# The first 1024 rows of x laid out as parts of 256 and 768 rows instead of one part, with a store for each

## The chip, the cores and the metric

The kernel runs on one core of one Trainium2 chip. The metric is device time in microseconds (us) of one execution; several runs are taken and their median is given. A profiled execution has, beside its time, a span: the time from the first to the last instruction that the profile shows.

## The reference

```python
def setup_inputs():
    batch, seq, d_model, r = 16, 512, 768, 16
    ...
        "x": np.random.randn(batch, seq, d_model).astype(np.float32),
        "A": np.random.randn(d_model, r).astype(np.float32) * 0.1,
        "B": np.random.randn(r, d_model).astype(np.float32) * 0.1,
        "scale": 0.5,

def reference(x, A, B, scale):
    lora = np.matmul(np.matmul(x, A), B)
    return (x + scale * lora).astype(np.float32)
```

x has 16 x 512 = 8192 rows of 768 floats: 25.17 MB that must be read, and as much that must be written. A and B are 48 KB each.

## The kernel before, in words

**Tiles, parts and groups.** A tile is 128 rows of x, one for each partition. There are 64 tiles. `PARTS` (L14) says how they lie in memory: a part of S tiles is a run of 128 x S rows of x, and partition p holds the rows p*S to p*S+S-1 of that run (`memory`, L96). One partition's share of a part is thus one contiguous run of S x 3072 bytes, and the shares of neighbouring partitions follow each other. A transfer of n of the S tiles takes n x 3072 bytes out of each share. The parts are 8, 8, 16, 16 and 16 tiles. In the core's memory the buffer `x_sb` has room for 48 tiles (`ROOM`, L61), and the last part takes the place of the first two (`tiles`, L103).

**Transfers.** `LOADS` (L106) and `STORES` (L128) list them as (part, first tile, tiles). There are eight loads: of part 0 the first 2 tiles (load 0) and then the other 6 (load 1), part 1 whole (load 2), part 2 in two halves (loads 3 and 4), part 3 whole (load 5), and part 4 in two halves (loads 6 and 7). There are five stores, one for each part. All are issued by SyncE (`on_sync`, L135), whose queue is SP in the profile: loads 0 and 1, the small A and B, and loads 2 to 5 at the start. Then SP waits until the sums of group 1 are done and until the fifth pair of matrix products into `lora` is under way (L169), issues stores 0 and 1 back to back (L170 and L171), waits for the landing of store 0 (`s_out0`, L172), issues load 6 into the place that store 0 read, waits for store 1 (`s_out1`, L174) and issues load 7 into the place of store 1. The stores of parts 2, 3 and 4 follow, each when its last group is summed (L176 to L178).

**Work on a group.** Eight tiles are a group; there are eight groups. ScalarE casts the first four tiles of a group to fp16 (`narrowed`, L182), GpSimd the other four; in group 0 GpSimd takes tiles 0 and 1, which load 0 brings, and ScalarE the others, which load 1 brings. VectorE transposes the group in 32 x 32 blocks (L246), TensorE multiplies by A (`projected`, L277), ScalarE scales the small product and spreads it (L234), TensorE multiplies by B (`raised`, L298), and VectorE adds the result to x in place (`summed`, L251), two tiles in each of 32 additions. `STORED` (L130) lists the group after which each store may leave; the waits on `s_sum` are counted by it. The order on each engine is that of the program, with counting semaphores between the engines. A semaphore that a transfer raises gets 16 from it.

**The end.** GpSimd waits for all the sums (L339) and for the last three stores (L341, 16 for each), and then clears the semaphores.

Of the kernel before, what the change touches and what calls it, by code (L numbers as in the profile page):

```python
# [10 lines left out]

PARTS = [8, 8, 16, 16, 16]  # L14


GROUP = 8
# [11 lines left out]
def kernel(  # L29
# [8 lines left out]
    nc = tc.nc  # L38
# [9 lines left out]
    NC = D // 64  # L48
    NG = sum(PARTS) // GROUP
    PAIRS = GROUP // 2  # L50
    assert sum(PARTS) * P == T and NG * GROUP == sum(PARTS)
    sc = float(scale)


    def sb(name, shape, dtype):
        return nc.alloc_sbuf_tensor(name, shape, dtype).ap()
# [3 lines left out]

    ROOM = sum(PARTS[:-1])  # L61
    x_all = sb("x_sb", [P, ROOM, D], fp32)
# [20 lines left out]
    def sem(name):  # L83
        sems.append(nc.alloc_semaphore(name))
        return sems[-1]
# [4 lines left out]
    tok = 0  # L90
    for i, S in enumerate(PARTS):
        parts.append(tok)
# [3 lines left out]
    def memory(t2, i, s, n):  # L96
        S = PARTS[i]
        return t2[ds(parts[i], S * P), :].rearrange("(p s) d -> p s d", s=S)[:, ds(s, n), :]

    def held(i, s, n):  # L100
        return tiles(where.index((i, s)), n)

    def tiles(t, n):  # L103
        return x_all[:, ds(t % ROOM, n), :]

    LOADS = [  # L106
        (0, 0, 2), (0, 2, 6), (1, 0, 8), (2, 0, 8), (2, 8, 8), (3, 0, 16), (4, 0, 8), (4, 8, 8)
    ]
    s_load = [sem(f"s_load{k}") for k in range(len(LOADS))]

# [12 lines left out]
    s_out0, s_out1 = sem("s_out0"), sem("s_out1")  # L123

    s_sum, s_out = sem("s_sum"), sem("s_out")

    MMS = 2 * NC
    STORES = [(0, 0, 8), (1, 0, 8), (2, 0, 16), (3, 0, 16), (4, 0, 16)]  # L128

    STORED = [where.index((i, s + n - 1)) // GROUP for i, s, n in STORES]  # L130

    section = ExitStack()
    section.enter_context(tc.tile_critical(no_gpsimd_drain=True))  # L133

    def on_sync(e):  # L135
        def load(k):
            ld = LOADS[k]
            e.dma_start(out=held(*ld), in_=memory(x2, *ld)).then_inc(s_load[k], 16)  # L138

        def summed(k):  # L140
            e.wait_ge(s_sum, k + 1)
            if STORED[k] + 1 < NG:

                e.sem_inc(s_free[PAIRS - 1], 1)

        def store(k, done):
            st = STORES[k]
            e.dma_start(out=memory(out2, *st), in_=held(*st)).then_inc(done, 16)

        load(0)  # L150
        load(1)
        e.wait_ge(s_ready, 1)
        blocks = A.rearrange("(c e) r -> c (e r)", e=64)
        for c in range(SETS):
            e.dma_start(
                out=a_rows[c : SET * SET : SET, :], in_=blocks[ds(c * SET, SET), :]
            ).then_inc(s_a, 16)
        e.wait_ge(s_brows, 1)
        e.dma_start(out=b_rows[0 : R * APART : APART, :], in_=B).then_inc(s_b, 16)
        for k in range(2, len(LOADS) - 2):  # L160
            load(k)

        for p in range(2, PAIRS):
            e.sem_inc(s_free[p], 1)
        summed(0)
        summed(1)


        e.wait_ge(s_lora, 2 * PAIRS + 2)  # L169
        store(0, s_out0)  # L170
        store(1, s_out1)  # L171
        e.wait_ge(s_out0, 16)  # L172
        load(len(LOADS) - 2)
        e.wait_ge(s_out1, 16)  # L174
        load(len(LOADS) - 1)
        for k in range(2, len(STORES)):  # L176
            summed(k)
            store(k, s_out)  # L178

    here = set()  # L180

# [55 lines left out]
    def on_vector(e):  # L237
# [10 lines left out]
        def summed(g, p):  # L248
            xs = tiles(g * GROUP + 2 * p, 2)
            e.wait_ge(s_lora, g * PAIRS + p + 1)  # L250
            ins = e.tensor_tensor(out=xs, in0=xs, in1=lora[p % 2], op=mybir.AluOpType.add)  # L251
            if p + 1 == PAIRS and g in STORED:
                ins.then_inc(s_sum, 1)
# [15 lines left out]
    def on_tensor(e):  # L269
# [57 lines left out]
        for p in range(PAIRS):  # L327
            raised(p)

    on_sync(nc.sync)  # L330
    on_gpsimd(nc.gpsimd)
    on_scalar(nc.scalar)
# [5 lines left out]

    nc.gpsimd.wait_ge(s_sum, len(STORED))  # L339
    nc.gpsimd.sem_clear(range(nums[0], s_sum.num))  # L340
    nc.gpsimd.wait_ge(s_out, (len(STORES) - 2) * 16)  # L341
    nc.gpsimd.sem_clear(range(s_sum.num, s_out.num + 1))
    section.close()

# [34 lines left out]
```

## Time and profile before

| | |
|---|---|
| median of 3 runs | 123.59 us (123.59 to 123.83) |
| the profiled execution | 123.66 us |
| its span | 121.8 us |
| VectorE busy | 81.8 us, 67% of the span |
| TensorE matmul busy | 52.8 us, 43% |
| ScalarE busy | 37.5 us, 31% |
| GpSimd busy | 28.4 us, 23% |
| bytes moved | 50.43 MB: 25.26 read from HBM, 25.17 written |

The profile divides the span into 40 equal slices and gives each engine's busy share in tenths; the row DMA is the mean busy share of the 16 DMA engines that serve the core. A packet is one contiguous piece of a transfer, on one DMA engine. The chain of waits follows the work back from the last instruction that an engine executed. The time from issue to landing of a transfer includes its stay in the queue behind other transfers.

### The profile page before, as it was taken

How to read it: one execution, taken by the hardware profiler on the slowest of the kernel's cores; microseconds unless marked ns; L12 is line 12 of the kernel's file. 1: busy time of each engine (PE TensorE's matmuls, PEld its weight loads, DVE VectorE, ACT ScalarE, POOL GpSimd, SP SyncE). 2: the span in 40 equal slices, each digit the busy share in tenths (PEclk: the TensorE clock that was granted, in tenths of full speed). 3: DMA queues.
4: the chain of work that ended last, by engine and by line, in shares of the span. 5: the costliest groups of instructions: out<-in, count | busy, mean ns of one | idle time of the engine just before them, and what ended most of it. 6: DMA issues, size and time to landing. Idle time of an engine off the chain costs nothing.

```text
span 121.8 us, 885 instructions
## 1 busy us (share of the span) xinstructions
PE 52.8 (43%) x322; PEld 31.0 (25%) x322; DVE 81.8 (67%) x42; ACT 37.5 (31%) x43; POOL 28.4 (23%) x24
## 2 busy tenths in 40 slices
PE   0000239487457547746745736994474540000000
PEld 0000026254233324424423312662233310000000
DVE  0002950699999999999999979969998795000000
ACT  4003938535408402835340093534004000000000
POOL 7731647135008002605300080530000000000000
PEclk9999999999999999999999995589999999555555
DMA  3999999999997996999999999997997998998990
GB/s 56 426 436 422 452 428 411 452 428 411 500 500 339 452 516 299 436 428 436 452 403 436 436 420 436 468 500 323 468 516 339 436 516 371 403 516 371 403 516 0
DMA packets 1928, 50.43 MB, mean 414 GB/s; under 512 B 236, under 2 KB 236, under 8 KB 392
## 3 DMA queue, kind: packets, MB, share of 16 engines
q1 hardware_dynamic: 1928, 50.43, 96.9%
HBM read 25.26 MB, written 25.17 MB: 414 GB/s over the span
## 4 chain that ended last, share of the span: by engine, by line
DVE 50%; PE 14%; issue 8%; DMA 8%; ACT 3%; SPq 0%
DVE x_sb L251 32%; DVE xt L246 18%; PE ps_yt L277 8%; DMA x_sb<-in_x_dram 8%; PE lora_ps L298 5%; ACT xn L190 3%; SPq L138 0%; SPq L374 0%; SPq L133 0%
## 5 line engine op out<-in xcount | busy, mean ns | idle before, releaser
L251 DVE TENSOR_TENSOR x_sb<-x_sb,lora_ps 128x1536 f32<-128x1536 f32 x32 | 53.8, 1737 | 2.5 <-PE lora_ps L298 2.5
L298 PE MATMUL lora_ps<-b_mm,y_bd 128*128 128x512 f16 (+1 forms) x128 | 26.3, 342 | 22.4 <-issue 13.4
L190 ACT CAST xn<-x_sb 128x3072 f16<-128x3072 f32 (+1 forms) x9 | 23.4, 2609 | 36.7 <-DMA x_sb<-in_x_dram 24.1
L277 PE MATMUL ps_yt<-xt,w_bd 128*128 128x256 f16 x192 | 27.3, 297 | 11.6 <-DVE xt L246 11.6
L190 POOL CAST xn<-x_sb 128x3072 f16<-128x3072 f32 (+1 forms) x8 | 20.7, 2588 | 45.3 <-DMA x_sb<-in_x_dram 23.0
L246 DVE STREAM_TRANSPOSE xt<-xn 128x3072 f32<-128x3072 f32 (+1 forms) x9 | 27.1, 3008 | 6.2 <-PE ps_yt L277 5.3
L277 PEld LDWEIGHTS ps_yt<-xt,w_bd 128*128 128x128 f16 x192 | 19.6, 104 | 20.0 <-issue 14.7
L298 PEld LDWEIGHTS lora_ps<-b_mm,y_bd 128*128 128x128 f16 x128 | 11.3, 101 | 35.5 <-issue 18.2
L234 ACT ACTIVATE y_bd<-ps_yt 32x256 f16<-32x256 f32 x32 | 12.0, 375 | 19.2 <-PE ps_yt L277 18.9
L239 DVE STREAM_TRANSPOSE a_t<-a_rows 32x1024 f32<-32x1024 f32 x1 | 2.0, 1965 | 11.5 <-DMA a_rows<-in_A_dram 11.5
L310 PE MATMUL lora_ps<-b_half,pick 128*128 128x512 f16 (+1 forms) x2 | 0.8, 504 | 12.8 <-POOL b_half L208 12.8
L310 PEld LDWEIGHTS lora_ps<-b_half,pick 128*128 128x128 f16 x2 | 0.1, 103 | 12.8 <-issue 12.8
L216 POOL COPY w_bd<-w_one 32x384 f16<-32x384 f16 x4 | 2.0, 502 | 0.2
L208 POOL CAST b_half<-b_rows 128x768 f16<-128x768 f32 x1 | 0.8, 829 | 4.7 <-DMA b_rows<-in_B_dram 4.7
L190 ACT ACT_TABLE_LOAD x1 | 1.3, 1283 | 0.9 <-SPq L133 0.9
L198 POOL MEMSET w_bd<- 128x1536 f32 x1 | 1.4, 1373 | 0.0
L210 POOL CAST w_one<-a_t 32x384 f16<-32x384 f32 x1 | 0.9, 852 | 0.9 <-DVE a_t L239 0.9
L195 POOL MEMSET a_rows<- 32x1024 f32 x1 | 0.9, 942 | 0.5 <-SPq L133 0.5
L227 ACT CAST b_mm<-lora_ps 128x768 f16<-128x768 f32 x1 | 0.8, 799 | 0.0
L196 POOL MEMSET b_rows<- 128x768 f32 x1 | 0.7, 728 | 0.0
L199 POOL MEMSET y_bd<- 128x512 f32 x1 | 0.5, 516 | 0.0
L201 POOL TENSOR_SCALAR_AFFINE_SELECT pick<-pick 128x128 f16<-128x128 f16 x1 | 0.3, 300 | 0.0
(5 smaller groups left out, 0.6 us busy)
## 6 DMA issues: line engine op xcount, KB each, us to landing
out_dram<-x_sb SPq DMA_DIRECT2D x3, 6144.0 KB, 22.3
x_sb<-in_x_dram SPq DMA_DIRECT2D x5, 3072.0 KB, 14.6
x_sb<-in_x_dram SPq DMA_DIRECT2D x1, 6144.0 KB, 41.8
out_dram<-x_sb SPq DMA_DIRECT2D x2, 3072.0 KB, 14.3
x_sb<-in_x_dram SPq DMA_DIRECT2D x1, 2304.0 KB, 9.8
x_sb<-in_x_dram SPq DMA_DIRECT2D x1, 768.0 KB, 4.6
a_rows<-in_A_dram SPq DMA_DIRECT2D x3, 16.0 KB
b_rows<-in_B_dram SPq DMA_DIRECT2D x1, 48.0 KB, 7.7
```

The costliest lines, as they stand in the source:

```text
L190: ins = copy(out=xn[:, ds(first, n), :], in_=tiles(t, n))
L195: e.memset(a_rows[0:Q], 0.0).then_inc(s_ready, 1)
L198: e.memset(w_bd.rearrange("p c k m -> p (c k m)").bitcast(fp32), 0.0)
L210: e.tensor_copy(out=w_one.rearrange("i (c e) k r -> i c e (k r)", c=SETS), in_=a_t[0:Q].rearrange("i k r (e c) -> i c e (k r)", c=SET)[:, ...
L216: e.tensor_copy(out=w_bd[ds(b * Q, Q), :, :, ds(b * Q, R)], in_=w_one).then_inc(s_w, 1)
L234: last = e.mul(out=y_bd[q, :, q], in_=y_ps[q, :, :], mul=sc)
L239: e.transpose(out=a_t[0:Q].rearrange("i k r c -> i (k r) c"), in_=a_rows[0:Q].rearrange("c (i k r) -> c (k r) i", k=2, r=R),).then_inc(s_r ...
L246: return e.transpose(out=ts[0], in_=ts[1])
L251: ins = e.tensor_tensor(out=xs, in0=xs, in1=lora[p % 2], op=mybir.AluOpType.add)
L277: mm = e.matmul(y_ps, w_bd[:, c, k, :], xv[:, :, c, :, k], start=(m == 0), stop=(m == MMS - 1),)
L298: mms.append(e.matmul(t[:, k, ds(n0, w)], y_bd[:, 2 * p + k, :], b_mm[:, ds(n0, w)], start=True, stop=True,))
L310: last = e.matmul(lora[0][:, 0, ds(n0, w)], pick.rearrange("p b r -> p (b r)"), b_half[:, ds(n0, w)], start=True, stop=True,)
```

## The change

Part 0 becomes two parts: the 2 tiles that load 0 brings and the 6 that load 1 brings. There are six parts, so the numbers of the later ones go up by one; the tiles' places in `x_sb`, the groups, and the eight loads with their sizes and their order stay. The rows that a tile of the first eight stands for are others, and so are the addresses in HBM that these transfers touch: load 0 reads one run of 768 KB and load 1 one of 2304 KB, where both took pieces of 6 KB and 18 KB out of shares of 24 KB. The store of part 0 becomes two, of 6 tiles and of 2 tiles, issued in this order, both counted on `s_out0`; SP waits for 32 there before load 6. The store of the next 8 tiles is issued right behind the two, as before behind one. What the first two stores wait for is one entry of `STORED`, so the counts on `s_sum` are as before.

```diff
-PARTS = [8, 8, 16, 16, 16]
+PARTS = [2, 6, 8, 16, 16, 16]
...
     LOADS = [
-        (0, 0, 2), (0, 2, 6), (1, 0, 8), (2, 0, 8), (2, 8, 8), (3, 0, 16), (4, 0, 8), (4, 8, 8)
+        (0, 0, 2), (1, 0, 6), (2, 0, 8), (3, 0, 8), (3, 8, 8), (4, 0, 16), (5, 0, 8), (5, 8, 8)
     ]
...
-    STORES = [(0, 0, 8), (1, 0, 8), (2, 0, 16), (3, 0, 16), (4, 0, 16)]
+
+    STORES = [(1, 0, 6), (0, 0, 2), (2, 0, 8), (3, 0, 16), (4, 0, 16), (5, 0, 16)]
 
     STORED = [where.index((i, s + n - 1)) // GROUP for i, s, n in STORES]
+    assert STORED[0] == STORED[1]
+    STORED = STORED[1:]
...
         e.wait_ge(s_lora, 2 * PAIRS + 2)
         store(0, s_out0)
-        store(1, s_out1)
-        e.wait_ge(s_out0, 16)
+        store(1, s_out0)
+        store(2, s_out1)
+        e.wait_ge(s_out0, 32)
         load(len(LOADS) - 2)
         e.wait_ge(s_out1, 16)
         load(len(LOADS) - 1)
-        for k in range(2, len(STORES)):
+        for k in range(2, len(STORED)):
             summed(k)
-            store(k, s_out)
+            store(k + 1, s_out)
...
-    nc.gpsimd.wait_ge(s_out, (len(STORES) - 2) * 16)
+    nc.gpsimd.wait_ge(s_out, (len(STORES) - 3) * 16)
```

## The prediction

> **What bounds the kernel now.** I read the slices and the DMA queue first, since 50.43 MB in a span of 121.8 us is a mean of 414 GB/s.
>
> ```profile
> DMA  3999999999997996999999999997997998998990
> DMA packets 1928, 50.43 MB, mean 414 GB/s; under 512 B 236, under 2 KB 236, under 8 KB 392
> q1 hardware_dynamic: 1928, 50.43, 96.9%
> ```
>
> The 16 DMA engines are busy for 96.9% of the span: from the second slice to the last but one nothing is left over. A share of 96.9% is 118.0 us, so only 3.8 us of the span, lead and tail together, lie outside. The stretches say whether the rate differs between reading and writing (columns: the stretch and its length, busy time and instructions of PE, PEld, DVE, ACT, POOL, granted clock, DMA share, GB/s).
>
> ```profile
> 2.00:4.00 2.00, 0.00 (x0) 0.00 (x0) 0.00 (x0) 0.20 (x1) 2.00 (x4) 1.00 0.88 255
> 10.00:18.00 8.00, 1.48 (x6) 0.64 (x7) 5.40 (x3) 4.93 (x3) 3.69 (x6) 1.00 1.04 442
> 47.50:55.50 8.00, 4.29 (x28) 2.37 (x26) 8.00 (x5) 4.25 (x5) 2.75 (x1) 1.00 1.02 439
> 0.00:121.80 121.80, 52.85 (x322) 30.99 (x322) 81.85 (x42) 37.48 (x43) 28.45 (x24) 0.90 0.97 414
> ```
>
> Loads run at 442 GB/s (10 to 18 us), stores at 439 (47.5 to 55.5): the same ceiling. Only the start is slower, 255 GB/s from 2 to 4 us, though the engines are 88% busy there: the first packets of load 0 take long. Third comes the chain of waits, in order of time; its last two pieces:
>
> ```profile
> 95.32 0.02 issue
> 95.34 6.75 DVE x_sb L251 x4
> ```
>
> The chain gives DVE 50% of the span, but it ends at 102.09 us, where the last store leaves. What follows, 20 us, is a transfer. SP's own line of time shows how late that issue is:
>
> ```profile
> 44.42 0.82 SPq L148 DMA_DIRECT2D out_dram<-x_sb  x2
> 55.26 7.75 SPq L138 DMA_DIRECT2D x_sb<-in_x_dram  x2
> ...
> 102.12 0.33 SPq L148 DMA_DIRECT2D out_dram<-x_sb  x1
> ```
>
> The packet records of the trace, set from the start of the span, have the first packet of the last store at 104.99 us and its last end at 120.46. Load 0 was issued at 0.97 and its first packet ran at 1.98, so an issue needs 1.0 us to become a packet; the last store could have run at 103.1 and stood 1.9 us in the queue. Even at the end VectorE has 1.9 us to spare. The time is thus 1.98 us of lead, 118.5 us of packets without a gap, 1.3 us of tail, and 1.86 us that the profiled execution (123.66) has outside its span. Only what changes the packets' time, or opens a gap, counts.
>
> **What a packet costs.** Each transfer of x has 128 packets, 8 for each DMA engine. By the packet records their medians are 234 ns for 6 KB (load 0), 686 for 18 KB (load 1), 912 for 24 KB (store 0), 1815 for 48 KB (last store). From 24 to 48 KB, 24,576 bytes cost 903 ns; 24 KB by that rate leave 9 ns of fixed cost, and 9 + 677 = 686 and 9 + 226 = 235 fit the small ones. A packet that raises a semaphore takes 9 ns too.
>
> **The change, part by part.**
>
> The loads. Number, size and order are as before; only addresses in HBM differ. The steady 6 KB packet already runs at 234 ns, the ceiling less 9 ns, though it is cut out of shares of 24 KB; so a contiguous run gives nothing there. What is left is the start: the mean of load 0's 128 packets is 316 ns, 82 over the steady one, 8 x 82 = 0.66 us for each engine. Of the first 16 packets 13 take 490 to 996 ns, with nothing ahead of them; of the last 64 nearly all take 234. If the old addresses cause this, 0.66 us is saved; if the new ones are as much worse, 0.66 us is lost. I take 0, because most of the excess stands in the first packet of an engine, which has nothing to overlap with at any address. Load 1 (mean 692 against 686) has 0.05 us to give.
>
> The stores. 128 packets of 24 KB become 128 of 18 KB and 128 of 6 KB: 686 + 234 - 912 = 8 ns for each partition, 0.064 us for an engine's eight, and one more semaphore packet, 0.009: **+0.07 us**. No store of 6 KB packets is in this trace. The low end is a packet without fixed cost, 0. The high end is load 0's mean for all of them: (316 + 692 - 912) x 8 = 0.77 us. I take the steady value, since stores of 24 KB (912) and loads of 24 KB (916) are within 4 ns.
>
> The third issue on SP. Three issues stand where two took 0.82 us, so the store of the next 8 tiles is issued 0.41 us later, at 45.24 instead of 44.83. Ahead of it stand the two new stores, 8 x (686 + 234) = 7.4 us of packets, and the end of load 5: it costs nothing. Without that cover it would cost 0.41 us. Behind it on SP is only the wait for `s_out0`.
>
> The wait for 32. It ends when the 2 tiles have landed, 0.07 us later than 55.26. Load 6 hangs on it, then load 7 and the later stores. Behind the awaited bytes the queue holds the 8-tile store, 8 x 912 ns = 7.3 us, which hides the new packets' 0.07 us and the issue. If that cover were gone, issue to packet would cost 1.0 us. Load 6 gates the casts of group 6:
>
> ```profile
> 69.91 2.75 ACT L190 CAST xn<-x_sb 128x3072 f16<-128x3072 f32 x1 [7.25 <-DMA x_sb<-in_x_dram]
> ```
>
> and VectorE waited 0.68 us for GpSimd's half of it, so the sums and the last issue are 0.07 us late too, out of a slack of 1.9.
>
> Sum: +0.07 us on 123.66 for the profiled kind of execution, **123.73**; on the median 123.59 (0.07 below the profiled one) **123.66 us**. No change that can be told: 0.2%, about 0.25 us, is what a measurement of this kernel can tell, and the three runs shown are 0.24 apart.
>
> A rule speaks against the new small store: the Trainium skill, "DMA: Bandwidth & Descriptors", section "Rules for kernel authors", asks for at least 1 MiB in a DMA, and its section "Anatomy of one DMA — SWDGE (gpsimd) path" fits 2.0 us fixed for each. By it one more DMA would give an estimate of 123.59 + 2.0 = 125.6 us, where the row above gives 0.07. The trace disagrees with it as a cost in a full queue: packets of load 1 start at 4.56 us while those of load 0 end until 5.26.
>
> **Rivals.**
>
> *The start gets slower* (slower). Neighbouring DMA engines, four partitions apart, read load 0 from addresses 24 KB apart instead of 96 KB. If the first packets collide more, the excess of 0.66 us doubles, all later packets move with it, and the time is 123.66 + 0.66 = 124.3 us. It decides from +0.25 us, when load 0's packets average about 345 ns. For it: the start is the only place below the ceiling. Against it: each engine has several packets in a row at 234 ns soon after.
>
> *The start gets faster* (faster). The same excess is due to the scattered rows and falls to between nothing and a half. Half gone: 123.66 - 0.33 = 123.3; all gone: 123.0. For it: later packets of load 0 too are at times 300 to 870 ns. Against it: those are few, and the steady ones show no cost of scatter.
>
> *The small store is slow* (slower). Its 6 KB packets cost load 0's mean, not 234: +0.77 us in all, 124.4 us. For it: no such write is seen, and the only 6 KB packets here were slow on the mean. Against it: those were at an idle queue, and these stand behind 18 KB packets.
>
> *Each DMA has a fixed price that shows* (slower). Issue to landing of load 0 is 4.6 us and its 786,432 bytes at 439 GB/s are 1.8, so 2.8 us are fixed. If the new landing exposed that, 126.4 us. Against it are the covers of 7.3 us above.
>
> ```profile
> out_dram<-x_sb SPq DMA_DIRECT2D x2, 3072.0 KB, 14.3
> x_sb<-in_x_dram SPq DMA_DIRECT2D x1, 2304.0 KB, 9.8
> x_sb<-in_x_dram SPq DMA_DIRECT2D x1, 768.0 KB, 4.6
> ```
>
> **How the numbers follow.** No change 0.46; faster start 0.25; slower start 0.16; slow small store 0.11; fixed price 0.02. So faster 0.25, same 0.46, slower 0.29. The start alone has 41% of the doubt because its excess has no explanation in the trace. The time is the likeliest case's, 123.66, with a range of its own from 123.4 to 123.9. The range over the cases goes from a start with most of its excess gone (123.66 - 0.56) to the two slower ones: 123.1 to 124.4. It leaves out a start wholly cured, both slower causes at once and the exposed price.
>
> **What would show it.** 2072 packets instead of 1928 (128 + 16 more), 252 under 512 B, 536 under 8 KB; DMA busy for 118.1 us of the span; the longest wait of SP for a store shorter by 0.34 us (0.41 less at its start, 0.07 more at its end); loads 6 and 7 issued from 55.3; 6 KB store packets at 234 ns. A rate in the stretch from 2 to 4 us far from 255 GB/s would be a changed start. I am wrong if a gap opens around 45 to 56 us, if those packets are slower, or if the last store is issued later than 104 us.

## The result, and the profile after

The changed kernel takes 124.51 us (median of 9 runs, 124.36 to 125.17); the kernel before, run beside it, 123.81 (9 runs, 123.59 to 124.16). The ratio is 1.006 with a 95% interval of 1.004 to 1.0081: slower by about 0.7 us. The prediction was no change, 123.66, with a range up to 124.4.

The slices and the queue of the changed kernel:

```profile
DMA  3999999999999898999999999999999899899890
DMA packets 2072, 50.43 MB, mean 411 GB/s; under 512 B 252, under 2 KB 252, under 8 KB 536
q1 hardware_dynamic: 2072, 50.43, 96.6%
```

The packet counts are the forecast ones, 144 more, all under 8 KB. The span is 122.7 us instead of 121.8, and the DMA engines are still busy for 96.6% of it. So no gap has opened that would hold 0.9 us: the packets themselves take longer. SP's line of time shows nothing late in the issues:

```profile
43.87 1.32 SPq L151 DMA_DIRECT2D out_dram<-x_sb  x3
55.38 7.73 SPq L141 DMA_DIRECT2D x_sb<-in_x_dram  x2
63.23 38.12 SPq L151 DMA_DIRECT2D out_dram<-x_sb  x3
```

The last store is issued at 101.0 us, a microsecond earlier than before, and ends later. The stretches show where the packets lose. The two last columns are the DMA share and the GB/s; the GB/s divided by the share is the rate of the DMA engines while they are busy. The kernel before, around the three places where the queue goes from loading to storing or back, called turns here:

```profile
45.00:48.00 3.00, 2.15 (x16) 1.39 (x16) 3.00 (x3) 0.01 (x1) 0.00 (x0) 1.00 1.02 434
60.00:63.00 3.00, 1.33 (x12) 0.84 (x11) 3.00 (x3) 1.50 (x4) 0.00 (x0) 1.00 0.97 410
74.00:78.00 4.00, 3.68 (x14) 1.98 (x15) 4.00 (x3) 0.66 (x2) 0.40 (x1) 0.50 1.04 430
```

The changed kernel, the start and the same three places:

```profile
2.00:4.00 2.00, 0.00 (x0) 0.00 (x0) 0.00 (x0) 0.19 (x1) 2.00 (x4) 1.00 0.88 326
45.00:48.00 3.00, 2.32 (x16) 1.39 (x16) 3.00 (x3) 0.00 (x0) 0.00 (x0) 1.00 0.75 309
60.00:63.00 3.00, 1.33 (x9) 0.54 (x7) 3.00 (x2) 1.50 (x4) 0.00 (x0) 1.00 1.01 401
74.00:78.00 4.00, 2.97 (x21) 1.81 (x22) 4.00 (x3) 0.34 (x1) 0.00 (x0) 1.00 1.10 412
```

The start is faster: 326 GB/s where it was 255. But a busy DMA engine's rate falls at each turn: from 434/1.02 = 425 to 309/0.75 = 412, from 423 to 397, and most around 76 us, from 413 to 375. The packet records say how much that is. The table gives, for each DMA engine, the time that its eight packets of a transfer take beyond the steady price (235 ns for 6 KB, 686 for 18, 913 for 24, 1816 for 48), and where the last engine ends; each kernel was profiled twice.

```
us over the steady price     before   again   after   again
load 0                        0.65     0.63    0.27    0.44
load 1                        0.05     0.04    0.12    0.09
load 5 (turn A, 45 us)        0.05     0.27    0.17    0.13
8-tile store (turn B, 60 us)  0.03     0.12    0.19    0.22
load 7 (turn C, 75 us)        0.16     0.25    0.56    0.70
packets of all, us          118.05   118.37  118.49  118.76
end of the last engine      120.46   121.03  121.42  121.53
```

All other transfers stay within 0.06 of their price. Apart from the start, the slow packets are the last ones ahead of a turn: in load 7 of the changed kernel 22 packets of 128 take up to 1651 ns instead of 913. On the mean of two profiles the packets take 0.41 us more for each engine, and the last engine falls behind by another 0.3: 0.7 us, the measured loss.

### The profile page after: what moved, and what is told of

It is laid out like the page before. It is cut to its first block, busy times and chain, and to the rows that moved or that the text cites. A ratio compares the mean times of both kernels' runs of the same rounds, so it can differ in the third digit from the quotient of the medians.

```text
span 122.7 us, 886 instructions
## 1 busy us (share of the span) xinstructions
PE 50.4 (41%) x322; PEld 29.5 (24%) x322; DVE 81.7 (67%) x42; ACT 37.5 (31%) x43; POOL 28.4 (23%) x24
## 3 DMA queue, kind: packets, MB, share of 16 engines
q1 hardware_dynamic: 2072, 50.43, 96.6%
## 4 chain that ended last, share of the span: by engine, by line
DVE 33%; DMA 29%; PE 9%; issue 4%; ACT 3%; POOL 2%; SPq 1%; DVEq 0%
DVE x_sb L255 21%; DMA x_sb<-in_x_dram 20%; DVE xt L250 12%; DMA out_dram<-x_sb 9%; PE ps_yt L281 6%; ACT xn L194 3%; PE lora_ps L302 3%; POOL xn L194 2%; SPq L141 0%; SPq L151 0%; SPq L378 0%; DVEq L268 0%; SPq L136 0%
## 5 line engine op out<-in xcount | busy, mean ns | idle before, releaser
L302 PE MATMUL lora_ps<-b_mm,y_bd 128*128 128x512 f16 (+1 forms) x128 | 25.0, 327 | 24.4 <-issue 15.9
L281 PE MATMUL ps_yt<-xt,w_bd 128*128 128x256 f16 x192 | 25.7, 286 | 11.4 <-DVE xt L250 11.4
L281 PEld LDWEIGHTS ps_yt<-xt,w_bd 128*128 128x128 f16 x192 | 18.8, 101 | 19.1 <-issue 14.6
L302 PEld LDWEIGHTS lora_ps<-b_mm,y_bd 128*128 128x128 f16 x128 | 10.5, 97 | 37.3 <-issue 17.9
```

The source lines that it names most:

```text
L281: mm = e.matmul(y_ps, w_bd[:, c, k, :], xv[:, :, c, :, k], start=(m == 0), stop=(m == MMS - 1),)
L302: mms.append(e.matmul(t[:, k, ds(n0, w)], y_bd[:, 2 * p + k, :], b_mm[:, ds(n0, w)], start=True, stop=True,))
```

## The experiments

Theories that the runs are to tell apart are named S, L and so on in the expectations.

**The split store alone, the new loads alone.** First kernel: the old parts and loads, with

```diff
-    STORES = [(0, 0, 8), (1, 0, 8), ...
+    STORES = [(0, 2, 6), (0, 0, 2), (1, 0, 8), ...
```

> Old parts and loads; only the first store is split into 6 and 2 tiles, now pieces of 18 KB and 6 KB out of shares of 24 KB. Theory S (the split store brings the loss, through the packets around the later turns between loading and storing): 124.3 to 124.6 us, and the 24 KB packets of load 7 average over 960 ns as in the changed kernel (983), not 933 as before. Theory L (the new addresses of the first loads bring it, by shifting the DMA engines against each other from the start on): within 0.15 us of the kernel before, load 7 near 933 ns, because the split itself costs 0.07 us.

Second: loads 0 and 1 from contiguous runs, the stores as before.

```diff
-in_=memory(x2, *ld)
+in_=run(x2, k) if k < 2 else memory(x2, *ld)
```

> The first 8 tiles are loaded as two contiguous runs, as in the changed kernel, but leave as one store in shares of 24 KB, so 1024 rows of the output stand in other places. Theory L: 124.3 to 124.6 us, load 7 over 960 ns. Theory S: no slower than before, 123.3 to 123.8 us, since load 0's packets average 269 ns instead of 316, 0.38 us less for each DMA engine; load 7 near 933 ns.

Measured: the split store 124.19 us, ratio 1.0023 (1.0008 to 1.0038); the new loads 124.71, ratio 1.0066 (1.0043 to 1.0089). Load 7 of the first lies 0.27 us over its price, of the second 0.82. So the loads alone bring as much as the whole change, as theory L has it, though load 0's packets got quicker. The split store's own packets cost what was forecast, 0.06 us for each engine: 234 ns for 6 KB, 687 for 18 KB. But the kernel with the split alone is 0.23% slower, 0.28 us, where theory L allowed 0.15. Its trace has 0.25 us at turn A, about what the second trace of the kernel before has, and no run shows where the rest of its loss lies. The two losses don't add up to that of the change. The stretch around turn C of the second kernel, at 387/1.10 = 352:

```profile
74.00:78.00 4.00, 3.05 (x14) 1.63 (x15) 4.00 (x2) 0.83 (x3) 0.00 (x0) 0.69 1.10 387
```

**Both kernels once more**, for second traces.

> The kernel before once more, for a second trace. If the slow packets at the turns are a trait of the kernel, load 7 averages 915 to 950 ns again and all packets together take 118.0 to 118.2 us for each engine. If they are chance of one execution, the mean of load 7 may as well be near 980.

> The changed kernel once more, for a second trace. If a trait: load 7 at 960 to 1000 ns, 118.4 to 118.6 us of packets for each engine, and the last engine about 1 us behind the median one. If chance: load 7 near 930 and the loss elsewhere.

They took 124.08 and 124.59 us and are the columns "again" above. Turn C looks like a trait, on two traces each: 0.16 and 0.25 before, 0.56 and 0.70 after. But the kernel before moves too. Its second execution issued the stores at 43.87 us instead of 44.42 and lost 0.27 us at turn A, not 0.05; its packets took 118.37 us, above what I expected.

**The turn without the other transfer in the queue.** In the changed kernel SP waits for load 7 before it issues the next store.

```diff
         load(len(LOADS) - 1)
+        e.wait_ge(s_load[len(LOADS) - 1], 16)
```

> The changed kernel, with SP waiting for load 7's landing before it issues the store of the next part, so that no store stands in the queue while load 7 ends. Theory M (the last packets before a turn are slow because the DMA engines that are done already move the next transfer the other way): load 7's mean falls from 983 and 1001 ns to 912 to 920, no packet over 1000 ns; a gap of 1 to 2 us opens behind it, of which the 0.6 to 0.7 us saved pays a part: 124.9 to 126.0 us. Rival R (they are slow from something else at that time, VectorE or the place read): load 7 stays over 960 ns, and the time is 125.5 us or more.

132.32 us, ratio 1.0647 (1.0589 to 1.0705), a miss of mine: SP also releases TensorE's buffers in `summed`, so VectorE stood still from 67 to 80 us, and the run couldn't tell M from R. Load 7 had no slow packet. The mended form puts the wait behind that release:

```diff
             summed(k)
+            if k == 2:
+                e.wait_ge(s_load[len(LOADS) - 1], 16)
             store(k + 1, s_out)
```

> The changed kernel, with the store of the part behind load 7 issued only when load 7 has landed, but SP's release to TensorE, which the earlier form of this held back too, given at its usual time: the sums run on while load 7 ends. Theory M (packets ahead of a turn are slow because the queue already holds the transfer the other way): load 7's mean 912 to 920 ns, none over 1000, and the turn between loads and stores costs a gap of 1 to 2.5 us instead of 0.6 us: 125 to 126.5 us. Rival R (VectorE's and the other engines' work slows them): over 960 ns.

125.54 us, ratio 1.0126 (1.0091 to 1.0162); load 7's mean is 912.3 ns, its slowest packet 922, with VectorE at work throughout:

```profile
74.00:76.00 2.00, 0.87 (x4) 0.52 (x5) 2.00 (x1) 1.01 (x3) 0.00 (x0) 0.80 0.91 393
76.00:78.00 2.00, 2.00 (x8) 0.96 (x7) 2.00 (x2) 0.00 (x0) 0.00 (x0) 0.50 0.20 86
```

The rate while busy is 432, and the gap stands behind it. Theory M holds this far: the last packets of load 7 are slow only when the store already stands in the queue behind them, and the other engines' work doesn't slow them.

**Load 0 alone, load 1 alone** contiguous. In these two some rows are read twice and others not at all.

```diff
+in_=run(x2, k) if k == 0 else memory(x2, *ld)     (the other: k == 1)
```

> The kernel before, with load 0 alone reading a contiguous run of 768 KB; load 1 reads its old pieces, so some rows are read twice and some not at all. Theory P0 (what counts is the first packets: the quicker start sets the DMA engines against each other in another way): 124.3 us or more, load 7 over 960 ns. Theory P1 (it is load 1's addresses): as before, 123.6 to 123.9 us, load 7 near 940 ns.

> The kernel before, with load 1 alone reading a contiguous run of 2304 KB, load 0 its old pieces. Theory P1: 124.3 us or more, load 7 over 960 ns. Theory P0: as before, 123.6 to 123.9 us, load 7 near 940 ns.

Load 0 alone: 124.26 us, ratio 1.0026 (1.0000 to 1.0053), load 7 at 972 ns. Load 1 alone: 123.83 us, ratio 1.0000 (0.9973 to 1.0027), load 7 at 951. They point to the first transfer, as P0 has it, but weakly: the two intervals overlap, and load 0 alone costs only four tenths of what both do together. In its trace load 0 gains 0.34 us of packets and load 1 loses 0.33.

**The standing of the DMA engines.** By standing I mean how far the 16 engines are apart in the queue. The semaphore packets behind loads 2, 3 and 4 show it: in the traces of the two kernels the first and the last engine are 0.7 to 0.8 us apart at 18 us, and as far apart at 32 us, so the start sets it. I changed it first by loading A in one transfer, so that it puts one packet on each of 12 engines instead of three on each of four:

```diff
-        for c in range(SETS):
-            e.dma_start(out=a_rows[c : SET * SET : SET, :], in_=blocks[ds(c * SET, SET), :]...
+        e.dma_start(out=a_rows[0:NC, :], in_=blocks).then_inc(s_a, 16)
```

> The kernel before, with the small A in one transfer of 12 rows instead of three of 4 rows: each of the three puts a 4 KB packet on four DMA engines only. If what the turns cost hangs on how the DMA engines stand to each other (P0 in the wide sense), this moves it too, in either direction, by 0.2 us or more on load 7's packets or the end. If only the first loads' addresses count, the turns stay as before and the time falls by at most 0.3 us, the two packets less on the busiest engines.

> The changed kernel, with the small A in one transfer of 12 rows instead of three of 4. Theory P (what counts is how the DMA engines stand to each other after the start, not the addresses): the turns change again, load 7's mean falls below 950 ns, and the time to 124.2 us or less. Rival A (the contiguous addresses as such): load 7 stays over 960 ns, 124.4 us or more.

> The changed kernel with A in one transfer, once more, for a second trace. If its quick turns were its trait: load 7 again below 960 ns, the 24 KB store near 914, the last packets of load 5 near 1819. If chance: one of them back at the changed kernel's values (load 7 983 to 1001, the store 937 to 940, load 5 1832 to 1837).

On the kernel before: 124.15 us, ratio 1.0014 (0.9991 to 1.0037); 0.5 us is lost on load 2, and turns A and C cost 0.03 and 0.17. The turns hardly moved, against the expectation. On the changed kernel: 124.07 us, ratio 1.0023 (1.0006 to 1.0041). Its load 0 is quick, and its turns are cheap: A, B and C cost 0.03, 0.01 and 0.25, in the second trace 0.09, 0.01 and 0.30. So the addresses as such don't make the turns dear. But that second execution took 124.54 us, as long as the changed kernel: both traces lose 0.47 and 0.42 us on load 2, and their packets take 118.53 and 118.49 us for each engine, no less than the changed kernel's. With A in one transfer the change costs a difference of ratios of 0.0009, 0.1 us, close to what I forecast for it; the two intervals overlap.

**A small transfer ahead of load 0**, to take the slow first packets off it with the old addresses.

```diff
+        e.dma_start(out=xt[:, 0, 0:256].bitcast(fp32), in_=x2[0:P, 0:128]).then_inc(s_warm, 16)
         load(0)
```

> The kernel before with its old addresses, and ahead of load 0 a small transfer of 128 pieces of 512 bytes that nothing uses (VectorE waits for it once, at the start). It takes the slow first packets upon itself, so load 0's packets should average below 280 ns (316 before), as in the changed kernel. Its own cost is one issue, 0.4 us, and 0.1 to 0.3 us of packets. Theory P (a quick load 0 sets the engines so that the turns cost more): load 7's mean over 960 ns, 124.6 us or more. Rival A (the contiguous addresses as such): load 7 at 930 to 950 ns, 124.1 to 124.5 us.

It couldn't tell the theories apart: load 0's packets averaged 337 ns, not below 280, so the start was no quicker. 124.92 us, ratio 1.0079 (1.0049 to 1.0108). Of this, 2.4 us of the profiled execution lie outside the span, where other kernels have 1.8; that I can't explain. It does show that the slow packets of load 0 aren't only the first of an idle queue: with pieces 24 KB apart they stay slow, and a contiguous run cures part of it.

**The standing wiped out.** In both kernels the first stores are issued only when load 5 has landed, so that all engines run dry and start together.

```diff
-        e.wait_ge(s_lora, 2 * PAIRS + 2)
+        e.wait_ge(s_load[len(LOADS) - 3], 16)
```

> The changed kernel, with the first stores issued only when load 5 has landed, so that all DMA engines run dry once and start the stores together. Theory P (the loss is carried by how far the DMA engines stand apart since the start): load 7's mean falls from 983 and 1001 ns to below 930, and the engines end within 0.4 us of each other instead of 1.6; the gap itself costs 1.5 to 2 us, so 124.6 to 125.4 us, within 0.2 us of the unchanged kernel treated in the same way. Rival N (not the standing of the engines but the contiguous run at the start, in some other way): load 7 over 960 ns, 0.5 us or more behind the unchanged kernel treated so.

> The kernel before with the same wait for load 5's landing. Theory P: load 7 below 930 ns, ends within 0.4 us, 124.5 to 125.3 us, at most 0.2 us from the changed kernel so treated. Rival N: the same here, but 0.5 us or more ahead of it.

126.77 us for the changed kernel, ratio 1.0225 (1.0194 to 1.0255), and 126.71 for the unchanged one, 1.0227 (1.0196 to 1.0257). So treated, the two kernels differ by 0.06 us, which counts against rival N, though the intervals would allow about 0.5 us. But the rest of my expectation was the wrong way round: the turns got dearer, not cheaper. At turn B, to which the engines came 0.15 us apart, it cost 0.77 and 0.74 us; at turn C, 0.50 and 0.24 apart, 1.02 and 0.86, with up to 38 slow packets. Turn A, whose stores were issued after the load had landed, cost 0.03 in both. The changed kernel so treated, around its turn C, at 393/1.15 = 342:

```profile
77.00:80.00 3.00, 3.00 (x13) 1.62 (x12) 3.00 (x3) 0.00 (x0) 0.00 (x0) 0.50 1.15 393
```

**The store issued in time.** If the queued store makes the turn dear, it should be issued just before it is needed. Load 7 is cut in two, and the landing of the first piece lets the store go; on the kernel before with 5 and 3 tiles and with 6 and 2, on the changed one with 6 and 2:

```diff
-(4, 8, 8)
+(4, 8, 6), (4, 14, 2)
...
             summed(k)
+            if k == 2:
+                e.wait_ge(s_load[len(LOADS) - 2], 16)
```

> The kernel before, with load 7 cut into 5 and 3 tiles, and the store behind it issued when the 5 have landed: about 2.2 us before the last packet, where it otherwise stands in the queue 12 us ahead. Theory M: no store in the queue until shortly before the turn, so the 24 KB row's slow packets (0.16 and 0.25 us for each DMA engine in the two traces of before) fall under 0.1, and no gap opens; 123.3 to 123.7 us. Against it: the three parts' own packets cost 0.15 us more, and a gap of the size of the gain leaves it at 123.8 or above.

> As the kernel with 5 and 3 tiles, but 6 and 2: the store is issued about 0.9 us later. If a store queued 2 us ahead still slows the last packets, this one has fewer slow packets than that with 5 and 3; if not, it only has the longer gap, up to 0.6 us, and is the slower one by that.

> The changed kernel, with load 7 cut into 6 and 2 tiles and the store behind it issued when the 6 have landed. If the slow packets of that turn are most of the change's loss (0.4 us for each DMA engine, and the late ends that they leave), the time falls from 124.5 to 123.6 to 123.9 us, at most 0.35 us over the unchanged kernel with the same edit (123.50): the split store's 0.07 and the dearer end of the 24 KB store, 0.13, stay. If the loss is somewhere else, it stays over 124.2 us.

5 and 3: 123.65 us, ratio 0.9984 (0.9968 to 0.9999). 6 and 2: 123.50 us, ratio 0.9981 (0.9967 to 0.9996), the fastest kernel of all, by 0.2%. Changed kernel: 123.99 us, ratio 1.0015 (1.0000 to 1.0031), instead of 1.006. In all three the pieces of load 7 lie within 0.04 us of their price. The issue of the kernel before with 6 and 2, and its stretch around turn C, at 492/1.16 = 424:

```profile
75.02 25.91 SPq L148 DMA_DIRECT2D out_dram<-x_sb  x3
```

```profile
74.00:78.00 4.00, 4.00 (x18) 2.29 (x18) 4.00 (x3) 1.12 (x1) 1.01 (x1) 0.57 1.16 492
```

The first packet of that store runs at 75.91 us, 0.9 us after its issue, just when the first engine is done with load 7: no gap, although 144 packets were added. The changed kernel falls by 0.45% with this edit, but the unchanged one falls by 0.19% too. So 0.26 of the change's 0.60% goes with turn C, and 0.34%, 0.42 us, stays, more than the 0.35 us I allowed; the intervals are too wide to say which share is larger. Its turn A shows why, at 276/0.71 = 389:

```profile
45.00:48.00 3.00, 2.32 (x16) 1.39 (x16) 3.00 (x2) 0.00 (x0) 0.00 (x0) 1.00 0.71 276
```

There it lost 0.43 us in this execution, and 0.15 at turn B.

**When the first stores are issued.** Turn A differs between traces of the same code, and one thing goes with it that none of the runs above was made to test: how early SP issues the first stores. The earliest and one of the latest, the first try of "the turn without the other transfer" and the changed kernel with A in one transfer:

```profile
43.36 1.31 SPq L151 DMA_DIRECT2D out_dram<-x_sb  x3
44.78 1.75 SPq L151 DMA_DIRECT2D out_dram<-x_sb  x3
```

The first cost 0.97 us at turn A, the second 0.03. Of the 17 traces with stores issued ahead of turn A, the six with an issue at 44.33 us or later cost 0.03 to 0.13 us there, the eight from 43.69 to 44.06 cost 0.09 to 0.44, and the three from 43.36 to 43.58 cost 0.25, 0.80 and 0.97. Every packet of load 5 over 1900 ns ends after that issue. The five traces whose code up to turn A is the changed kernel's issue at 43.36 to 44.33 us and pay 0.13 to 0.97; the four with the code of the kernel before issue at 43.85 to 44.49 and pay 0.05 to 0.27. So the change may also cost time by letting its first stores be issued earlier. No run moves that issue by a part of a microsecond with all else equal, so this isn't shown. At turn C it is hardly the reason: there the store is issued 12.7 to 13.4 us before its first packet in all four traces of the two kernels.

## Why the prediction was wrong, point by point

**Right.** The DMA queue bounds the kernel. The packet counts, the price of the split store's packets (0.06 us measured, 0.064 forecast), the third issue hidden on SP, the wait for 32 that ends 0.1 us later (55.38 against 55.26): all as worked out. The rival with a fixed price of 2.8 us for each DMA is out: the kernel with the split store alone, which has one DMA more, took 0.28 us longer. By the Trainium skill's fit ("DMA: Bandwidth & Descriptors", section "Anatomy of one DMA — SWDGE (gpsimd) path") one more DMA would be 2.0 us; this run doesn't bear that out for a full queue.

**The loads, taken at 0.** The start did change, as the rival "the start gets faster" has it: load 0's excess fell from 0.64 to 0.36 us on the mean of two profiles. My reason for 0, that the slow first packets are slow at any address, was wrong: the excess of the first 16 packets fell from 0.46 to 0.29 us for each engine. (Of those 16, 14 took 490 ns or more in the trace of before, not 13.) But the 0.28 us did not reach the end.

**The step that failed** is the one that made the time a sum of rigid pieces: lead, "118.5 us of packets without a gap" and tail, where "only what changes the packets' time" counts and packets are priced by size. Each rival moved "all later packets" by what the start gained or lost. In fact the last packets ahead of a turn can cost far more than their price when the next transfer already stands behind them: in load 7 of the changed kernel 21 and 29 packets of 128 took over 1000 ns, and with the store held back none passed 922. The sum had no term for this, and the change made it larger, mainly by way of its loads. Turns B and C went from 0.08 and 0.21 us (means of two) to 0.21 and 0.63, and the last engine fell another 0.3 us behind the mean. The trace of before already had this term: load 7 averaged 933 ns against 914 to 918 in the other 24 KB transfers, and I took the medians, which hide it.

The slower rivals gave 124.3 and 124.4, near the measured time, by mechanisms that didn't happen: the start got faster, and the small store is at its steady price. That they came near is luck.

**Open.** How the new loads make the turns dearer is argued, not shown. That it is the standing of the engines rests on the two kernels that become equal when the first stores wait for load 5, and on the one with A in one transfer. For turn A both fit as well with the time at which the stores are issued, since both moved that too. Which standing would make a turn dear isn't settled either: ahead of turn C the changed kernel's engines are 0.93 and 0.75 us apart, those before 0.74 and 1.23; and 0.50 apart cost 1.02 us in one kernel where 0.61 cost 0.17 in another. And why a store in the queue slows the load ahead of it, whose slow packets begin 2.1 us before the store's first packet in the changed kernel (74.08 and 76.23 us), no run shows.

## What to carry to other kernels

A full DMA queue isn't a rigid sum: the last packets before it goes from loading to storing can take twice their time and more when the next transfer already stands behind them, so look at means and maxima of the packets there, not at medians, and in more than one execution. Issue a transfer the other way one to two microseconds before it is needed, by the landing of all but the last piece of what runs ahead of it: 0.9 and 1.7 us ahead left no slow packet here. A change at the start of a queue that never runs dry can be paid for 40 to 70 us later.

## What the runs showed of the hardware that I had not expected

- A store queued early slows the last packets of the load ahead of it: 24 KB packets of 912 ns reached 1651 ns, in the kernel with the new loads alone 2389; held back, none passed 922. In the changed kernel's first trace the store was queued for 13 us, but only packets that began in the last 2.1 us before its first one took over 1000 ns.
- DMA engines that reached a turn 0.15 us apart lost 0.74 and 0.77 us each, against 0.03 to 0.22 for engines 0.8 to 1.4 us apart at the same turn B of the two kernels. At turn C the rule doesn't hold throughout.
- What turn A costs goes with how early the store is issued: 0.03 to 0.13 us with an issue at 44.33 us or later, 0.80 and 0.97 with one at 43.58 and 43.36.
- Pieces of 6 KB out of 24 KB cost about 0.3 us on a first load over a contiguous run (load 0's means: 316 and 313 ns against 269 and 290), and a small transfer ahead of it doesn't cure that (337 ns).
- One more transfer in a full queue costs next to nothing in its own packets: 9 ns for each packet and 9 for the semaphore, 0.06 us for each engine in all.
